# Seven products of quarter matrices for an input projection, with weight sums made by accumulating DMAs

## The chip, the core and the metric

The kernel runs on one NeuronCore of a Trainium2 chip. The metric is the device time of one execution in microseconds (us). Before the change it is 662.69 us, the median of 3 runs (662.54 to 663.6). The profile is one further execution.

TensorE (PE) multiplies: a matmul takes a stationary 128x128 operand, loaded ahead of it, and streams a moving operand of up to 512 columns through it into PSUM. VectorE (DVE), ScalarE (ACT) and GpSimd (POOL) work on tiles in SBUF; the first two can read PSUM as well. DMA queues move data between HBM and SBUF; the queue of SyncE (SP) issues nearly all of them here.

## The reference

One layer over 512 tokens of width 1024, float32. All ten inputs of the two branches and gates come out of one projection of 1024 x 10240:

```python
h = rms_norm(x, norm_gain[layer])
proj = jnp.einsum('bsd,dc->bsc', h, w_in[layer])
(sb_q, sb_k, sb_v, sb_g, r_q, r_k, r_v, r_g, m_sb, m_ret) = jnp.split(proj, SPLIT_POINTS, axis=-1)

qa = rms_norm(split_heads(sb_q, SB_HEADS), sb_q_gain[layer])
ka = rms_norm(split_heads(sb_k, SB_HEADS), sb_k_gain[layer])
va = split_heads(sb_v, SB_HEADS)
out_a = merge_heads(stick_breaking_attention(qa, ka, va)) * jax.nn.silu(sb_g)

qb = rotary(split_heads(r_q, RET_HEADS))
kb = rotary(split_heads(r_k, RET_HEADS)) * (RET_KEY_DIM ** -0.5)
vb = split_heads(r_v, RET_HEADS)
ret = chunkwise_retention(qb, kb, vb)
ret = rms_norm(ret, ret_out_gain[layer][None, :, None, :])
out_b = merge_heads(ret) * jax.nn.silu(r_g)

p_a = jnp.einsum('bsw,wd->bsd', out_a, w_branch_sb[layer])
p_b = jnp.einsum('bsw,wd->bsd', out_b, w_branch_ret[layer])
merged = (jax.nn.sigmoid(m_sb + b_merge[layer, 0]) * p_a
          + jax.nn.sigmoid(m_ret + b_merge[layer, 1]) * p_b)
x = x + jnp.einsum('bsd,de->bse', merged, w_out[layer])
```

## The kernel before, in words

Every large product is computed in three passes: each float32 operand is split into a high part (a copy in the rounded type float32r, on ScalarE) and a low part (the difference, on VectorE), and hi x hi, hi x lo and lo x hi are summed in PSUM (`split`, lines 114 to 116; `mm3`, lines 91 to 95).

The input projection is cut into 20 **groups** of 512 columns: four for queries and keys (`qk`, two heads each), two each for the attention values (`v`), its gate (`sg`), the retention's values (`rv`) and gate (`rg`) and the two merge gates (`ma`, `mb`), and four for the retention's queries and keys (`rqk`, one head each). Six more groups of the same size are the two branch projections (`pa`, `pb`) and the output projection (`fin`). All 26 go through `dense` (line 211): over eight blocks of 128 input rows, four PSUM banks, three passes, so 96 matmuls of 512 columns. `load_split` (line 191) brings the weights in four pieces of 128x1024 per group: a load on SP's queue into one of two raw buffers, a cast on ScalarE and a subtraction on VectorE into one of two pairs of `whi` and `wlo` buffers, all at high priority. The token operand `xT` is made and split once, at the start (line 145).

Attention and retention are generators whose small matmuls are put between those of the groups: `work.step()` in `dense` counts down and resumes them (class `Interleaver`, line 40). So PE's order is fixed by the program; a scheduler orders the other engines by priority, and each engine then runs its instructions in that order.

Behind each group its four PSUM banks are read out: `qk_group` (line 285), `v_group` (line 330), `silu_group` (line 343), `gate_group` (line 357) and `rope_group` (line 429). The calls from line 523 on set the order of the groups.

Of the kernel before, what the change touches and what calls it, by code (L numbers as in the profile page):

```python
# [12 lines left out]
P = 128  # L13
S = 512
# [15 lines left out]
V_ROOM, M_ROOM = 66, 112  # L30


RAW_BUFS = 2
V_BUFS = 14
N_IDLE = 8
# [32 lines left out]
def hybrid_block(ctx, tc, x, x_t, vecs, w_in, w_a, w_b, w_o, cos_t, sin_t, decay, out):  # L68
# [34 lines left out]
    def G_tile(name):  # L103
        return big.tile([P, S], F32, tag="G", bufs=8, name=name)

    def O_pair(name):
        return [big.tile([P, S], F32R, tag="O", bufs=16, name=f"{name}_{q}") for q in range(2)]
# [33 lines left out]
    vec = const.tile([P, V_ROOM], F32, name="vec")[:, :V_N]  # L141
    xT_hi = const.tile([P, NK, S], F32R, name="xT_hi")
    xT_lo = const.tile([P, NK, S], F32R, name="xT_lo")

    def first_loads():

        raws = [wpool.tile([P, 2, S], F32, tag="raw", bufs=RAW_BUFS, name=f"first_raw{k}") for k in range(2)]
        xt = [T_tile(f"xt{hf}", F32) for hf in range(2)]
        for k in range(NK):
            ks = slice(k * P, (k + 1) * P)  # L150
            if k < 4:
                load_weights(raws[k // 2][:, k % 2 : k % 2 + 1, :], w_in, k, 1, ((C_Q, 256), (C_K, 256)))
            load(xt[k // 4][:, k % 4, :], x_t[ks, :])
            if k == 0:
                load(vec, vecs)
        for k in range(NK):
            r = xt[k // 4][:, k % 4, :]
            g = vec[:, V_NG + k : V_NG + k + 1]
            nc.scalar.activation(xT_hi[:, k, :], r, AF.Copy, scale=g)  # L159
            nc.vector.scalar_tensor_tensor(  # L160
                xT_lo[:, k, :], r, g, f32(xT_hi[:, k, :]), op0=ALU.mult, op1=ALU.subtract
            )
        return raws

    first = first_loads()

    idle = const.tile([P, S], mybir.dt.bfloat16, name="idle")
    nc.vector.memset(idle, 0.0)
    pi = side_psum("pi")
    for j in range(N_IDLE):  # L170
        matmul(pi, idle[:, :P], idle, start=True, stop=True)

# [10 lines left out]
    m_half = const.tile([P, M_ROOM], F32, name="m_half")[:, :16]  # L183
# [7 lines left out]
    def load_split(name, w, blocks):  # L191
# [19 lines left out]
    def dense(name, act, w, blocks, rows):  # L211
# [4 lines left out]
        for k, hi, lo in load_split(name, w, blocks):  # L216
            if name == "fin1" and k >= NK - 2:
                late.append((k, act(k), (hi, lo)))
                continue
# [430 lines left out]
```

## Time and profile before

| what | value |
|---|---|
| median of 3 runs | 662.69 us (662.54 to 663.6) |
| the profiled execution, own time | 664.18 us |
| its span, first to last instruction | 662.4 us |
| PE busy / weight loads | 656.3 us (99%) / 546.4 us (82%) |
| VectorE, ScalarE, GpSimd busy | 375.9 us (57%), 260.7 us (39%), 50.8 us (8%) |
| matmuls (PE instructions) | 3096 |
| moved by DMA | 65.02 MB, 98 GB/s in the mean |

The span leaves out 1.78 us of the execution. Matmuls are pipelined and the profile models their ends, so a matmul's own length overlaps its neighbours'; the pace is read from the time that a run of them takes. The view of waits names, for an engine's idle time, what ended last. The chain that ended last follows the program back from its last instruction to what released each step.

### The profile page before, as it was taken

The page shows a single profiled execution, that of the slowest core. Times are in us where ns is not written, and L with a number is a line of the kernel's source. Part 1 is how long each engine was busy: PE and PEld are TensorE (multiplying, and loading weights), DVE is VectorE, ACT ScalarE, POOL GpSimd, SP SyncE. Part 2 cuts the span into 40 slices and gives each one's busy share as a digit, 9 for nine tenths or more (in the row PEclk, how much of TensorE's full clock was granted, in tenths as well). Part 3 has the DMA queues.
Part 4 walks back from the last instruction along what each step waited for, and adds up shares of the span by engine and source line. Part 5 has one row for each costly group of instructions (what it writes and reads, how often), then busy time and mean ns, then how long its engine had stood idle before and what let it go on. Part 6 is the DMA issues. An engine that isn't in the chain of part 4 may idle for free.

```text
span 662.4 us, 7979 instructions
## 1 busy us (share of the span) xinstructions
PE 656.3 (99%) x3096; PEld 546.4 (82%) x3096; DVE 375.9 (57%) x560; ACT 260.7 (39%) x416; POOL 50.8 (8%) x50
## 2 busy tenths in 40 slices
PE   8999999999999999999999999999999999999997
PEld 5888888888888888888888888888888888888886
DVE  6456874587497477632334763844862953544632
ACT  4744534464364554422312342433433443422310
POOL 0051000441000400000000001001001001000000
PEclk9999999999999999999999999999999999999999
DMA  8543223322322323233333323222323322335541
GB/s 288 189 128 96 65 63 96 96 64 65 95 64 64 96 63 96 60 99 96 95 96 111 96 64 106 84 80 81 96 70 106 93 66 64 96 95 161 158 159 63
DMA packets 42182, 65.02 MB, mean 98 GB/s; under 512 B 2848, under 2 KB 19488, under 8 KB 42144
## 3 DMA queue, kind: packets, MB, share of 16 engines
q1 hardware_dynamic: 41568, 63.47, 31.2%
q10 hardware_dynamic: 576, 1.05, 0.4%
q8 instruction: 24, 0.39, 0.3%
q14 instruction: 14, 0.11, 0.1%
HBM read 62.41 MB, written 2.10 MB: 97 GB/s over the span
## 4 chain that ended last, share of the span: by engine, by line
PE 99%; DMA 0%; SPq 0%; ACT 0%; DVE 0%; issue 0%; DVEq 0%; ACTq 0%
PE qk_ps L86 14%; PE rqk_ps L86 13%; PE sg_ps L86 7%; PE v_ps L86 7%; PE ma_ps L86 7%; PE rv_ps L86 7%; PE mb_ps L86 7%; PE rg_ps L86 7%; PE fin_ps L86 7%; PE pb_ps L86 7%; PE pa_ps L86 7%; PE po L86 2%; PE z L86 2%; PE rz L86 2%; PE ro L86 2%; PE pw L89 1%
## 5 line engine op out<-in xcount | busy, mean ns | idle before, releaser
L86 PE MATMUL qk_ps<-qk_hi,xT_hi 128*128 128x512 f32 x128 | 51.5, 411 | 0.9 <-ACT xT_hi L159 0.9
L86 PE MATMUL rqk_ps<-xT_hi,rqk_hi 128*128 128x512 f32 x128 | 50.5, 394 | 0.0
L86 PE MATMUL rqk_ps<-xT_hi,rqk_lo 128*128 128x512 f32 x128 | 50.0, 391 | 0.0
L86 PE MATMUL rqk_ps<-xT_lo,rqk_hi 128*128 128x512 f32 x128 | 50.0, 390 | 0.0
L86 PE MATMUL qk_ps<-qk_lo,xT_hi 128*128 128x512 f32 x128 | 49.8, 398 | 0.0
L86 PE MATMUL qk_ps<-qk_hi,xT_lo 128*128 128x512 f32 x128 | 49.5, 395 | 0.0
L86 PE MATMUL pb_ps<-ob,pb_hi 128*128 128x512 f32 x128 | 39.5, 390 | 0.0
L86 PE MATMUL pa_ps<-oa,pa_hi 128*128 128x512 f32 x128 | 39.4, 389 | 0.0
L116 DVE TENSOR_TENSOR rqk_lo<-rqk_raw,rqk_hi 128x1024 fp32r<-128x1024 f32 x16 | 20.8, 1300 | 23.9 <-ACT rqk_hi L115 23.9
L386 DVE TENSOR_TENSOR_SCAN keep<-keep,zero 128x128 f32<-128x128 f32 (+3 forms) x32 | 27.1, 847 | 7.3 <-ACT keep L384 7.3
L86 PEld LDWEIGHTS qk_ps<-qk_hi,xT_hi 128*128 128x128 f32 x128 | 24.5, 192 | 6.2 <-ACT xT_hi L159 1.8
L86 PEld LDWEIGHTS qk_ps<-qk_hi,xT_lo 128*128 128x128 f32 x128 | 24.5, 191 | 5.4
L189 POOL TENSOR_TENSOR rrr<-ms,m_half 128x4 f32<-128x4 f32 x4 | 4.0, 1007 | 316.3 <-DVE ms L188 316.3
L86 PEld LDWEIGHTS qk_ps<-qk_lo,xT_hi 128*128 128x128 f32 x128 | 24.7, 193 | 4.3
L86 PEld LDWEIGHTS rqk_ps<-xT_hi,rqk_lo 128*128 128x128 f32 x128 | 24.1, 188 | 5.0
L86 PEld LDWEIGHTS pb_ps<-ob,pb_hi 128*128 128x128 f32 x128 | 24.0, 188 | 5.0
L86 PEld LDWEIGHTS pa_ps<-oa,pa_hi 128*128 128x128 f32 x128 | 24.0, 188 | 5.0
L86 PEld LDWEIGHTS rqk_ps<-xT_hi,rqk_hi 128*128 128x128 f32 x128 | 24.1, 188 | 4.7
L86 PEld LDWEIGHTS rqk_ps<-xT_lo,rqk_hi 128*128 128x128 f32 x128 | 24.1, 188 | 4.6
L115 ACT CAST rqk_hi<-rqk_raw 128x1024 fp32r<-128x1024 f32 x16 | 16.8, 1050 | 25.8 <-PE rqk_ps L86 16.5
L116 DVE TENSOR_TENSOR qk_lo<-qk_raw,qk_hi 128x1024 fp32r<-128x1024 f32 x14 | 17.6, 1259 | 15.1 <-ACT qk_hi L115 15.1
L86 PE MATMUL v_ps<-v_hi,xT_hi 128*128 128x512 f32 x64 | 26.1, 408 | 0.0
(185 smaller groups left out, 1709.8 us busy)
## 6 DMA issues: line engine op xcount, KB each, us to landing
rqk_raw<-in_w_in SPq DMA_DIRECT2D x32, 256.0 KB, 3.0
qk_raw<-in_w_in SPq DMA_DIRECT2D x28, 256.0 KB, 3.0
v_raw<-in_w_in SPq DMA_DIRECT2D x8, 512.0 KB, 3.9
sg_raw<-in_w_in SPq DMA_DIRECT2D x8, 512.0 KB, 3.6
rv_raw<-in_w_in SPq DMA_DIRECT2D x8, 512.0 KB, 3.6
ma_raw<-in_w_in SPq DMA_DIRECT2D x8, 512.0 KB, 3.6
pa_raw<-in_w_a SPq DMA_DIRECT2D x8, 512.0 KB, 3.9
rg_raw<-in_w_in SPq DMA_DIRECT2D x8, 512.0 KB, 3.6
```

What stands on the lines that cost most here:

```text
L86: tc.keep_in_program_order(nc.tensor.matmul(*a, **k))
L89: tc.keep_in_program_order(nc.tensor.transpose(*a))
L115: nc.scalar.copy(hi, src)
L116: nc.vector.tensor_sub(lo, src, f32(hi))
L189: nc.gpsimd.tensor_tensor(dst, t[:, :width], m_half[:, :width], op=ALU.pow)
L386: nc.vector.tensor_tensor_scan(keep[:, :n][:, ::-1], keep[:, :n][:, ::-1], zero.broadcast_to([P, n]), 1.0, op0=ALU.mult, op1=ALU.add,)
```

## The change

Each of the 20 projection groups is cut in quarters: token halves (256), input halves (512) and column halves (256). Instead of eight products of quarters, `proj` makes seven products of sums (Strassen's scheme in Winograd's form); each product is 24 matmuls of 256 columns: four blocks of 128 rows, two halves of a PSUM bank, three passes.

- The token sums are made once at the start (`token_operands`): scalings by the norm gain on ScalarE and GpSimd, three sums on GpSimd and one on VectorE, seven splits.
- The weight sums are made for each group in SBUF by DMAs: three quarters are loaded on SP's queue, and four times a quarter is added onto a raw tile by an accumulating DMA that GpSimd issues (`add_from`). One raw tile holds in turn B11, B11+B12, B11+B12+B22 and B11+B12+B22+B21, another B22 and then B22+B12. Each of the seven operands is split into `whi` and `wlo`; there are now three buffers of each and four raw buffers, all 128x1024.
- Sums of products that share a bank go on accumulating in it: ScalarE copies the bank's state out (`kept`, three times a group), and VectorE combines (three times a group). The four result quarters are three SBUF tiles and a PSUM bank.
- The weights come to the chip cut in quarters, each with 4 KB in one piece per partition (`w_q`).
- The functions behind the groups read quarters instead of banks. The split pairs of the branch activations are no longer kept: `branch_act` splits each again for both column halves. The order of groups is changed: `sg1` ahead of `qk2`, both `ma` ahead of both `pa`, `rv0` behind them.

The groups `pa`, `pb` and `fin` keep their 96 matmuls of 512 columns.

```diff
+    def add_from(dst, src):
+        nc.gpsimd.dma_start(dst, src, accum_op=ALU.add)
...
+        s1, s3 = (G_tile(f"xs{j}").rearrange("p a (b t) -> p (a b) t", b=2) for j in range(2))
+        nc.vector.tensor_sub(s1, x21, x22)
+        act_pair("s1", s1)
+        s2, n4 = (G_tile(f"xt{j}").rearrange("p a (b t) -> p (a b) t", b=2) for j in range(2))
+        nc.gpsimd.tensor_sub(s2, s1, x11)
+        act_pair("s2", s2)
+        nc.gpsimd.tensor_add(n4, x12, s2)
+        act_pair("n4", n4)
+        nc.gpsimd.tensor_sub(s3, x11, x21)
...
+    def weight_pair(name, src, by_rows=False):
+        hi = wpool.tile([P, 4, H], F32R, tag="whi", bufs=3, name=f"{name}_hi")
+        lo = wpool.tile([P, 4, H], F32R, tag="wlo", bufs=3, name=f"{name}_lo")
...
+        with tc.high_priority():
+            if g == 0:
+                r = first
+            else:
+                r = raw_tile(f"{name}_raw1")
+                load(r, quarter(g, B11))
+            got = made(0, r)
+        yield got
+        with tc.high_priority():
+            add_from(r, quarter(g, B12))
+            got = made(1, r)
+        yield got
+        with tc.high_priority():
+            add_from(r, quarter(g, B22))
+            r2 = raw_tile(f"{name}_raw2")
+            load(r2, quarter(g, B22))
+            got = made(2, r)
+        yield got
+        with tc.high_priority():
+            got = made(3, r2)
+        yield got
+        with tc.high_priority():
+            add_from(r, quarter(g, B21))
+            add_from(r2, quarter(g, B12))
+            r3 = raw_tile(f"{name}_raw3")
+            load(r3, quarter(g, B21))
+            got = made(4, r2)
+        yield got
...
+    def product(ps, a, b, rows, first):
+
+        for k in range(4):
+            for j in range(2):
+                js, o = slice(j * P, (j + 1) * P), ps[:, j, :]
+                l, r = (a, b) if rows else (b, a)
+                for n, (u, v) in enumerate(((0, 0), (0, 1), (1, 0))):
+                    matmul(
+                        o, l[u][:, k, js], r[v][:, k, :], start=first and k == j == n == 0,
+                        stop=k == 3 and n == 2, skip_group_check=True,
+                    )
+            if k % 2 == 1:
+                work.step()
...
+        y, w = bank("y"), bank("w")
+        product(y, acts["x11"], next(ops), rows, True)
+        c11 = kept("c11", y)
+        product(w, acts["s1"], next(ops), rows, True)
+        c22 = kept("c22", w)
+        product(y, acts["s2"], next(ops), rows, False)
+        c12 = kept("c12", y)
+        product(w, acts["n4"], next(ops), rows, False)
+        nc.vector.tensor_sub(c12, w, c12)
+        product(y, acts["s3"], next(ops), rows, False)
+        with tc.high_priority():
+            nc.vector.tensor_sub(c22, c22, y)
+        q = bank("q")
+        product(q, acts["x12"], next(ops), rows, True)
+        nc.vector.tensor_add(c11, q, c11)
+        product(y, acts["x22"], next(ops), rows, False)
+        return {(0, 0): c11, (0, 1): c12, (1, 0): y, (1, 1): c22}
...
-    def proj(name, blocks, rows):
-        return dense(name, lambda k: (xT_hi[:, k, :], xT_lo[:, k, :]), w_in, blocks, rows)
```

How ScalarE's instructions move is shown at the group `rg0`, the retention's first gate. Before, from its first cast to its last; `rk`, `rm` and the `rqk_hi` made from `rm` are the read-out of the group ahead, `rg_raw` the landed weights:

```order
L115 CAST rg_hi_3067<-rg_raw_3065 128x1024 [waits DMAHW1_49,DVE_49,PE_49]
L436 COPY rk_0_3029<-rqk_ps_2901 128x512 [waits PE_49]
L115 CAST rg_hi_3099<-rg_raw_3097 128x1024 [waits DMAHW3_49,DVE_49,PE_49]
L436 COPY rk_1_3030<-rqk_ps_2902 128x512 [waits PE_49]
L115 CAST rqk_hi_3027<-rm_0_0_3033 128x512 [waits DVE_49]
L115 CAST rqk_hi_3027<-rm_0_2_3035 128x512 [waits DVE_49]
L115 CAST rg_hi_3129<-rg_raw_3127 128x1024 [waits DMAHW4_49,PE_49,Activation_49]
L115 CAST rqk_hi_3027<-rm_1_0_3047 128x512 [waits DVE_49]
L115 CAST rqk_hi_3027<-rm_1_2_3049 128x512 [waits DVE_49]
L115 CAST rg_hi_3181<-rg_raw_3179 128x1024 [waits DMAHW5_49,PE_49,Activation_49]
```

In the change, the same stretch; the digit behind `rg0_` is the operand, DMAHW a load of SP's queue, DMASW a DMA of GpSimd's:

```order
L120 CAST rg0_0_hi_4251<-rg0_raw1_4249 128x1024 [waits DMAHW1_49,DVE_49,PE_49]
L120 CAST rg0_1_hi_4284<-rg0_raw1_4249 128x1024 [waits DMASW0_49,DVE_49,PE_49]
L300 COPY rg0_c11_4281<-rg0_y_4247 128x512 [waits PE_49]
L120 CAST rqk_hi0_4213<-rm0_10_0_4215 128x2x256 [waits DVE_49]
L120 CAST rqk_hi0_4213<-rm0_00_0_4223 128x2x256 [waits DVE_49]
L300 COPY rg0_c22_4312<-rg0_w_4248 128x512 [waits PE_49]
L120 CAST rg0_2_hi_4317<-rg0_raw1_4249 128x1024 [waits DMASW1_49,Activation_49]
L120 CAST rg0_3_hi_4347<-rg0_raw2_4315 128x1024 [waits DMAHW3_49,Activation_49]
L120 CAST rqk_hi0_4213<-rm0_01_0_4231 128x2x256 [waits DVE_49]
L300 COPY rg0_c12_4345<-rg0_y_4247 128x512 [waits PE_49]
L120 CAST rqk_hi0_4213<-rm0_11_0_4239 128x2x256 [waits DVE_49]
L120 CAST rg0_4_hi_4380<-rg0_raw2_4315 128x1024 [waits DMASW3_49,Activation_49]
```

Four casts, each from its own load, have become seven (5 and 6 follow next), of which 1, 2, 4 and 6 stand behind a DMA that GpSimd issues; the copies out of PSUM stand between them.

GpSimd's queue held no DMA. Before, from the last query/key group's scalings to the first of the retention:

```order
L189 TENSOR_TENSOR rr_2011<-ms,m_half 128x16 [waits DVE_49]
L301 TENSOR_TENSOR rr_2011<-rr_2011,rx 128x16 [waits Pool_49]
L303 TENSOR_TENSOR qraw_0_1991<-qraw_0_1991,rr_2011 128x512 [waits PE_49,Activation_49,Pool_49]
L303 TENSOR_TENSOR qraw_1_1993<-qraw_1_1993,rr_2011 128x512 [waits PE_49,Activation_49]
L303 TENSOR_TENSOR qraw_2_1995<-qraw_2_1995,rr_2011 128x512 [waits PE_49,Activation_49]
L303 TENSOR_TENSOR qraw_3_1997<-qraw_3_1997,rr_2011 128x512 [waits PE_49,Activation_49]
L189 TENSOR_TENSOR rrr_3354<-ms,m_half 128x4 [waits DVE_49]
```

In the change, from the second addition of `sg1`, the group behind `qk1`, to the first of the next group:

```order
L154 DMA sg1_raw1_1403<-in_w_q 128x1024 [waits DMASW0_49,DVE_49]
L225 TENSOR_TENSOR rr1_1385<-ms_1390,m_half_169 128x16 [waits DVE_49]
L428 TENSOR_TENSOR rr1_1385<-rr1_1385,rx_171 128x4 [waits Pool_49]
L428 TENSOR_TENSOR rr1_1385<-rr1_1385,rx_171 128x4 x3
L431 TENSOR_TENSOR qraw1_1371<-qraw1_1371,rr1_1385 128x512 [waits Activation_49,Pool_49]
L431 TENSOR_TENSOR qk1_c11_1137<-qk1_c11_1137,rr1_1385 128x512 [waits PE_49,Activation_49,Pool_49]
L431 TENSOR_TENSOR qk1_c12_1227<-qk1_c12_1227,rr1_1385 128x512 [waits Activation_49,Pool_49]
L154 DMA sg1_raw1_1403<-in_w_q 128x1024 [waits DMASW1_49,DVE_49]
L154 DMA sg1_raw2_1469<-in_w_q 128x1024 [waits DMAHW2_49,DMASW7_49,DVE_49]
L431 TENSOR_TENSOR qk1_c22_1183<-qk1_c22_1183,rr1_1385 128x512 [waits Pool_49]
L154 DMA qk2_raw1_1699<-in_w_q 128x1024 [waits DMAHW4_49,DMASW6_49,DVE_49]
```

The additions wait for VectorE's subtractions (DVE) and for earlier additions of their own raw tile (DMASW), and stand in one row with the scalings of the query/key group ahead.

## Rows read from the trace of the kernel before

**Rows 1.** The page: span, busy time by engine, granted clock in 40 slices.

```profile
span 662.4 us, 7979 instructions
...
PE 656.3 (99%) x3096; PEld 546.4 (82%) x3096; DVE 375.9 (57%) x560; ACT 260.7 (39%) x416; POOL 50.8 (8%) x50
...
PEclk9999999999999999999999999999999999999999
```

**Rows 2.** The page: the chain that ended last, shares of the span by engine.

```profile
PE 99%; DMA 0%; SPq 0%; ACT 0%; DVE 0%; issue 0%; DVEq 0%; ACTq 0%
```

**Rows 3.** Groups of PE instructions by form: count, busy us, mean ns, idle us before.

```profile
L86 PE MATMUL qk_ps<-qk_hi,xT_hi 128*128 128x512 f32 x128 | 51.5, 411 | 0.9 <-ACT xT_hi L159 0.9
...
L86 PE MATMUL rqk_ps<-xT_hi,rqk_lo 128*128 128x512 f32 x128 | 50.0, 391 | 0.0
```

**Rows 4.** The chain in order of time: start us, length us, what.

```profile
53.38 4.08 PE sg_ps L86 x18
...
276.08 21.76 PE pa_ps L86 x96
...
363.12 12.24 PE rg_ps L86 x54
...
396.74 2.52 PE ro L86 x21
...
571.41 43.52 PE pb_ps L86 x192
```

**Rows 5.** Groups of ScalarE and VectorE instructions by form.

```profile
L116 DVE TENSOR_TENSOR rg_lo<-rg_raw,rg_hi 128x1024 fp32r<-128x1024 f32 x8 | 9.8, 1222 | 6.8 <-ACT rg_hi L115 6.8
...
L544 DVE TENSOR_TENSOR pa<-pa_ps,ma 128x512 f32<-128x512 f32 x8 | 5.5, 692 | 2.6 <-PE pa_ps L86 2.6
...
L115 ACT CAST rg_hi<-rg_raw 128x1024 fp32r<-128x1024 f32 x8 | 8.4, 1052 | 13.6 <-PE rqk_ps L86 8.8 <-PE rg_ps L86 4.9
...
L486 ACT COPY roraw<-ro 128x512 f32<-128x512 f32 x8 | 4.7, 585 | 23.7 <-PE ro L86 23.7
```

**Rows 6.** Timeline of one weight split in `rg`: start us, us, engine, what.

```profile
373.85 1.05 ACT L115 CAST rg_hi<-rg_raw 128x1024 fp32r<-128x1024 f32 x1 [1.24 <-PE rg_ps L86]
...
374.94 1.22 DVE L116 TENSOR_TENSOR rg_lo<-rg_raw,rg_hi 128x1024 fp32r<-128x1024 f32 x1 [1.60 <-ACT rg_hi L115]
```

**Rows 7.** DMA issues: count, KB each, median us from issue to landing.

```profile
rqk_raw<-in_w_in SPq DMA_DIRECT2D x32, 256.0 KB, 3.0
...
rg_raw<-in_w_in SPq DMA_DIRECT2D x8, 512.0 KB, 3.6
...
x<-in_x SPq DMA_DIRECT2D x2, 1024.0 KB, 8.6
```

**Rows 8.** Groups of GpSimd instructions by form.

```profile
L303 POOL TENSOR_TENSOR qraw<-qraw,rr 128x512 f32<-128x512 f32 x16 | 19.2, 1227 | 0.3
L189 POOL TENSOR_TENSOR rr<-ms,m_half 128x16 f32<-128x16 f32 x4 | 13.6, 3391 | 152.2 <-DVE ms L188 152.2
```

**Rows 9.** Two stretches: busy us of engines, granted clock, DMA share, GB/s.

```profile
6.00:12.00 6.00, 6.00 (x19) 4.74 (x19) 5.07 (x10) 2.90 (x5) 0.00 (x0) 1.00 0.96 341
...
363.00:580.00 217.00, 217.00 (x1056) 183.56 (x1055) 129.27 (x184) 82.79 (x118) 12.18 (x12) 1.00 0.28 84
```

**Rows 10.** Waits: engine, line, waited for; us in total, times, longest us.

```profile
ACT pb_hi L115 <- PE pb_ps L86: 17.5, 5, 4.4
```

**Rows 11.** Timeline of the start: the last split of a first weight piece.

```profile
10.94 0.69 DVE L205 TENSOR_TENSOR qk_lo<-first_raw,qk_hi 128x512 fp32r<-128x512 f32 x1
```

More of the change, by code (lines that the diff above doesn't have):

```diff
@@ L139, in hybrid_block, with raw_tile, quarter @@
     nc.scalar.activation(warm, zero, AF.Sigmoid)
[L141 to L167, printed above, removed]
+    vec = const.tile([P, V_N], F32, name="vec")
+    def raw_tile(name):
+        return wpool.tile([P, 4, H], F32, tag="raw", bufs=RAW_BUFS, name=name)
+    def quarter(g, q):
+        return w_q[g, q].rearrange("p (k c) -> p k c", k=4)
+    def add_from(dst, src):
+        nc.gpsimd.dma_start(dst, src, accum_op=ALU.add)
+    xt = [T_tile(f"xt{hf}", F32) for hf in range(2)]
+    first = raw_tile("first_raw")
+    load(vec, vecs)
+    for k in range(4):
+        load(first[:, k, :], quarter(0, B11)[:, k, :])
+        load(xt[0][:, k, :], x_t[k * P : (k + 1) * P, :])
+    load(xt[1], x_t[4 * P :, :].rearrange("(k p) t -> p k t", p=P))
+    idle = tmp.tile([P, 2 * S], mybir.dt.bfloat16, tag="tmp", name="idle")[:, :S]
     nc.vector.memset(idle, 0.0)
@@ L201, in load_split @@
[L201 to L207 removed]
+                raw = raw_tile(f"{name}_raw{k}").rearrange("p (a b) c -> p a (b c)", a=2)
+                load(raw, w[k * P : (k + 2) * P, c0 : c0 + S].rearrange("(a p) c -> p a c", p=P))
@@ L475, in retention @@
             yield 1
-        vv = v()
         for b2 in range(2):
@@ L533, in hybrid_block @@
-    sg[1] = silu_group("sg1", C_G + S)
-    qk_group(3)
-    work.add(attention((6, 7), lambda: 1 in sg, lambda: v[1], lambda: sg[1]))
-    rv[0] = v_group("rv0", C_RV)
-    pa = []
-    for g in range(2):
-        m = gate_group(f"ma{g}", C_MA + S * g, V_BM + 4 * g)
-        ps = dense(f"pa{g}", branch_act(oa), w_a, ((S * g, S),), False)
-        t = T_tile(f"pa{g}", F32)
+    sg[1] = silu_group("sg1", 4)
+    qk_group(2, 5)
+    work.add(attention((4, 5), lambda: 1 in sg and 1 in v, lambda: v[1], lambda: sg[1]))
@@ L543, in hybrid_block @@
+    v[1] = v_group("v1", 6)
+    qk_group(3, 7)
+    work.add(attention((6, 7), lambda: 1 in sg and 1 in v, lambda: v[1], lambda: sg[1]))
+    pa = [gate_group(f"ma{n}", 8 + n, V_BM + 4 * n) for n in range(2)]
+    for n in range(2):
+        ps = dense(f"pa{n}", branch_act(f"oa{n}", oa), w_a, S * n, False)
         for j in range(4):
-            nc.vector.tensor_mul(t[:, j, :], ps[j], m[j])
-        pa.append(t)
-    def ret(h):
-        rq = rope_group(h)
+            nc.vector.tensor_mul(pa[n][:, j, :], ps[j], pa[n][:, j, :])
```

372 lines of the change are left out of this document (217 added, 155 removed).

## Prediction

> **What bounds the kernel now.** I read the page's engine shares first, then the chain that ended last, then that chain in order of time. TensorE (PE) is busy 99% of the 662.4 us span at the full granted clock, 9 tenths in every slice [rows 1], and the chain lies on it for 99% [rows 2]: nothing but PE time counts today. The chain in order of time gives the price of a projection group: 96 matmuls of 512 columns take 21.76 us, 226.7 ns each [rows 4]. (The mean in the table of groups, 391 ns, is a modelled length of overlapping instructions, and no pace [rows 3].) The same view has a run of 256-column matmuls: 21 in 2.52 us, 120 ns each [rows 4]. So 256 columns more cost 106.7 ns, which leaves 13.3 ns that each matmul costs whatever its width.
>
> Next come the waits: ScalarE's casts wait for PE to give weight buffers back, 4.4 us at a time [rows 10]. Weights are ready early now, and the whole margin of the forecast is whether they still are. Last, the side work (attention, retention) between the groups. From 53.38 to 276.08 eight groups stand, 8 x 21.76 = 174.1 of 222.7 us: 6.1 us of side work each. From 363.12 to 571.41 eight more: 174.1 of 208.3, 4.3 us each [rows 4].
>
> **The change, part by part.** *PE.* Seven products of 24 matmuls replace 96 matmuls. A product is 24 x 120 ns = 2.88 us, a group 20.16 us: 1.60 us less, 32 us over 20 groups. An eighth of the columns would be 2.7 us; the 13.3 ns on 72 more matmuls takes back the rest. The six groups of the branch and output projections stay at 21.76.
>
> *ScalarE and VectorE.* A group has seven casts of 128x1024 where it had four, each 1.05 us, and seven subtractions at 1.22 [rows 5]; three copies out of PSUM at about 0.59 and three combinations at about 0.69 [rows 5]. The branch activations are split for each half of the columns, 16 more pairs. VectorE: 376 us [rows 1] + 60 x 1.22 + 60 x 0.69 + 16 x 0.69 = 501; ScalarE 261 + 63 + 35 + 10, less 12 copies that go (7), 362. Neither fills 640 us, so I cost them at nothing as throughput. They count as links in a chain.
>
> *The chain of a weight operand.* An accumulating DMA overwrites the quarter that was just split, so it may start only behind that split's subtraction, and the next cast starts only when it has landed. Call its time, from subtraction's end to landing, L. A cast and its subtraction take 2.31 us (373.85 to 376.16) [rows 6]; I take s = 2.55, since four times a group such a step queues behind VectorE work of around 0.7 us. Number the products 0 to 6. Operand n takes the buffer of operand n - 3, so operand 0 of a group waits for product 4 of the group before. From there:
> - **X**, from the end of product 4 to the start of the next group's product 2: split 0, add, split 1, add, split 2 = 3s + 2L. PE has products 5, 6, 0 and 1 to cover it, 11.52 us, and four sevenths of the side work.
> - **Y**, from the start of product 2 to that of product 4: operand 3 is a plain load, its subtraction ends 1.25 later, then add and split: 1.25 + s + L, against 5.76 us of products and two sevenths.
> - **Z**, product 4: 2.88 us and a seventh.
>
> The order of the instructions bears this out: cast 1 of a group stands on ScalarE right behind cast 0 with a wait for the DMA between, and the four additions go through GpSimd's queue in a row.
>
> *L.* No row of before shows an accumulating DMA. The nearest row is the plain load of the same 512 KB, 3.6 us [rows 7]. An addition reads its destination too. The table of DMA issues has 256 KB in 3.0 us and 512 KB in 3.6, so another 512 KB of reading is some 1.2 us: L = 4.8, my value. From below, a gain against 3.6 isn't excluded: the new layout gives each partition one 4 KB piece, where the loads of before go in pieces of 2 KB or 1 KB, and such a piece may travel better; I take 3.2. From above, a 1024 KB load lands in 8.6 us, at the crowded start [rows 7]. I keep to 4.8 because the stages in question are not crowded: from 363 to 580 the DMA engines are busy 28% at 84 GB/s, and they have reached 341 [rows 9].
>
> With L = 4.8, X = 17.25 and Y = 8.6. The covers with side work of 6.1 are 15.0 and 7.5; with 4.3, 14.0 and 7.0; with none, 11.5 and 5.8: the chain is later in every group. Group times are X + Y + Z: 29.6 in eight attention groups (237), 29.35 in eight retention groups (235), 28.75 in two without side work (58). The group behind the two pa projections finds its first operands made, and takes 11.5 + 8.6 + 2.9 = 23.
>
> *Start.* The first raw quarter is split by about 11 us (the last such subtraction ends at 11.6 now, twice as wide) [rows 11]. Then two additions and splits, Y and a product: 11 + 2(L + s) + 8.6 + 2.9 = 37.2 to the end of product 4. The sums of token quarters run beside it: four scalings on GpSimd at 1.23 or less [rows 8], a subtraction and a split end near 19, before the weights of product 2.
>
> *GpSimd.* Its queue now holds the additions among the query/key scalings: a power of 3.4 us and three products of 1.23 [rows 8] stand between the second and third addition of the groups behind the first two query/key groups. They end about when that third addition is wanted; I count nothing, and 2 us for each of the two go into the range.
>
> *Sum.* 37.2 + 237 + 235 + 58 + 23, products 5 and 6 of the last group (5.8), six unchanged groups (130.6), the tail behind the last matmul (3.9): 730 us of span, about **731** with the 1.8 us that this execution takes outside its span. That is 67 above the profiled 664.18, itself 1.5 above the median of 662.69; that difference lies in the range.
>
> By the Trainium skill (DMA: Bandwidth & Descriptors, Anatomy of one DMA) a DMA issued from GpSimd takes 2.0 us plus its bytes at 436 GB/s; an estimate by it is 3.2 us for 512 KB. The page's formula is for a plain DMA; no run here shows one from that engine, and the sum by it would be 650.
>
> **The rivals.** *1, faster: the additions land as quickly as a good load.* Each us of L is worth 58 us (three links in 18 groups, one in the group behind pa, three at the start). L = 3.6 gives 663, so that is the point: below it the change wins. At 3.2 the attention groups are bound by PE alone (15.0 + 7.5 + 3.75 = 26.25), the retention groups take 24.55, those without side work 24.0: 210 + 196 + 48 + 21.4 + 32.4 + 140.3 = 648, **650** with the rest. With no wait at all it would be 640. For it: the longer pieces and the idle DMA engines. Against it: the second stream that an addition reads.
>
> *2, slower still: an addition is far from a load,* through descriptors made by GpSimd's software or an adder below the engines' copy rate. L = 6 gives **801**, 8.6 gives 951. For it: nothing in these rows limits it; against it: the 28% DMA load.
>
> *3, the clock falls.* PE's only idle time in the main groups now is 0.9 us at the start [rows 3], and the clock stays at 2.4 GHz [rows 1]. The forecast leaves PE idle twice a group for 1 to 6 us. If the grant drops to 1.2 GHz, the 106.7 ns per matmul double: 2.6 us on a product. Product 4 is the one with no cover: 18 x 2.6 = 46, **777**. The Trainium skill (TensorE: Matmul & The Clock Gate, The HAM clock gate) has the throttled clock as the default that activity releases, which speaks against this change; the trace has no idle stretch long enough to agree or differ.
>
> *4, nothing moves:* stalls and the 32 us cancel (L near 3.6), **663**.
>
> **How the numbers follow.** Forecast, L between 3.7 and 5.6, 668 to 778: 0.46. Rival 1: 0.18. Rival 2: 0.20. Rival 3: 0.11. Rival 4: 0.05. The measurement can tell 0.2%, 1.3 us. Faster 0.18, same 0.05, slower 0.77. The range goes from 650, rival 1 at 3.2, to 850, where L would be 6.9: outside lie the best part of rival 1 and the far end of rival 2, about 0.2. The slower cases' own range is 668 to 850.
>
> **What would show it.** Right: PE's share near 88%, its idle time at the first matmul of products 2 and 4, released by ScalarE's cast or VectorE's subtraction; in the chain that ended last, GpSimd's DMAs with a share of a quarter or more; additions landing in 4 to 6 us; 256-column matmuls 120 ns apart inside a product. Wrong: an addition landing in under 3.6 us with PE still at 97% or more (rival 1); additions of 6 us and more (rival 2); a granted clock under 0.95 (rival 3); a pace above 120 ns, which would upset the 20.16; or stalls that end on a free PSUM or SBUF buffer, which I cost at nothing.

## The result, and the profile after

The changed kernel takes **877.35 us** (median of 4 runs, 874.45 to 878.61) against 662.62 for the kernel before: ratio 1.323, 95% interval 1.320 to 1.327. The forecast was 731, its range ended at 850. The direction was right, the size was not: 146 us are missing from the sum.

The page of the changed kernel: engine shares, PE and its granted clock in 40 slices, the GpSimd queue's share of the DMA engines, the chain that ended last, and the two kinds of 512 KB transfer (median us from issue to landing).

```profile
span 876.8 us, 11443 instructions
...
PE 707.8 (81%) x4536; PEld 656.5 (75%) x4536; DVE 500.8 (57%) x748; ACT 354.2 (40%) x583; POOL 142.2 (16%) x149
...
PE   4676797858978679699977868969778778888997
...
PEclk7686988979898799999998979979889897999999
...
q0 software_dynamic: 11520, 41.95, 27.8%
...
DMA 34%; PE 25%; issue 15%; DVE 12%; ACT 7%; POOL 6%; POOLq 0%; SPq 0%; ACTq 0%; DVEq 0%
...
rqk_raw<-in_w_q POOLq DMA_DIRECT2D x16, 512.0 KB, 5.4
...
rqk_raw<-in_w_q SPq DMA_DIRECT2D x12, 512.0 KB, 3.7
```

Where the chain was PE for 99% [rows 2], it now runs through DMAs for 34%, PE for 25%. PE falls from 99% [rows 1] to 81%, with stalls in nearly every slice, and the granted clock, 9 tenths throughout before, dips in most. VectorE's 500.8 us and ScalarE's 354.2 are the forecast's 501 and 362.

One group step by step, rqk0 to rg0, first ScalarE's casts of weights, then GpSimd's issues, both from the timeline (start, length, what ended the idle time before).

```profile
457.01 1.05 ACT L120 CAST rqk_hi<-rqk_raw 128x1024 fp32r<-128x1024 f32 x1 [3.82 <-PE rv_y L88]
...
464.99 1.05 ACT L120 CAST rqk_hi<-rqk_raw 128x1024 fp32r<-128x1024 f32 x1 [1.74 <-DMA rqk_raw<-in_w_q]
...
473.05 1.99 ACT L120 CAST rqk_hi<-rqk_raw 128x1024 fp32r<-128x1024 f32 x2 [2.18 <-DMA rqk_raw<-in_w_q]
...
483.52 2.94 ACT L120 CAST rqk_hi<-rqk_raw 128x1024 fp32r<-128x1024 f32 x3 [2.77 <-DMA rqk_raw<-in_w_q]
490.19 1.05 ACT L120 CAST rg_hi<-rg_raw 128x1024 fp32r<-128x1024 f32 x1 [3.73 <-PE rqk_y L88]
```

```profile
459.67 0.86 POOL L154 DMA_DIRECT2D rqk_raw<-in_w_q  x1 [15.28 <-DVE rqk_lo L121]
467.65 0.88 POOL L154 DMA_DIRECT2D rqk_raw<-in_w_q  x1 [7.11 <-DVE rqk_lo L121]
475.70 0.88 POOL L154 DMA_DIRECT2D rqk_raw<-in_w_q  x1 [7.17 <-DVE rqk_lo L121]
476.84 0.86 POOL L154 DMA_DIRECT2D rqk_raw<-in_w_q  x1 [0.26 <-issue]
```

This is the chain that the forecast drew. Cast 0 waits for product 4 (457.01). Its subtraction ends at 459.33, the addition is issued 0.34 us later and cast 1 can start at 464.99: L, from the subtraction to the cast that the landing releases, is 5.65 us, within 0.1 us the same at the second link, and 6.97 at the third, where the addition for operand 4 (476.84) stands behind one that only operand 6 needs (475.70). The stretches X, Y and Z of this group, as windows (from the end of product 4 to the end of split 2, to that of split 4, to the end of the next product 4; the bounds, then busy us of each engine, granted clock, DMA share, GB/s):

```profile
457.01:475.35 18.34, 12.79 (x98) 11.89 (x96) 8.31 (x14) 8.40 (x14) 1.75 (x2) 0.93 0.48 107
475.35:485.83 10.48, 8.11 (x48) 7.71 (x48) 3.06 (x4) 2.89 (x4) 1.74 (x2) 0.80 0.56 100
485.83:490.15 4.32, 4.27 (x23) 4.27 (x24) 2.27 (x2) 0.64 (x1) 0.00 (x0) 0.60 0.67 216
```

Forecast: 17.25, 8.6 and 3.5. In Z the clock is at 0.60 of 2.4 GHz: most of its matmuls start 213 ns apart instead of 120.

To compare kernels over all groups, I took X, Y and Z from the timeline by the starts of the first matmuls of products 2, 4 and 5 (18 groups; the first and the one behind pa left out; here side work that lies between two products counts to the stretch before it). A product's first matmul needs only the cast, so these bounds can lie 1.2 us ahead of those of the windows. Means in us:

```
                              X      Y      Z     sum   whole kernel
forecast                    17.25   8.6    3.55  29.4     731
changed kernel              19.4   11.35   4.9   35.7     877.35
e4 the same program again   19.1   11.1    4.8   35.1     866.0
e1 plain copies, GpSimd     16.2    9.1    4.65  30.0     761.86
e2 plain copies, SP         15.5    8.1    4.6   28.3     731.73
e3 no chain                 14.5    6.85   4.9   26.2     687.98
e5 PE kept busy             20.7   11.9    4.35  36.9     899.44
e8 VectorE adds two         14.9    7.2    4.9   27.1     704.90
e17 order of additions kept 22.75  12.1    4.9   39.8     946.91
```

The runs e1 to e11 and e17 are single runs. e4, described below, turned out to be the changed program once more, in the series of e1 to e3: against it the gains of these three are 11 us smaller than against 877.35.

The three links of the same 18 groups, from the subtraction's end to the landing, means in us:

```
                            first  second  third
forecast                     4.8    4.8     4.8
changed kernel               6.0    5.9     7.8
e4 the same program again    5.8    5.6     7.7
e1 plain copies, GpSimd      4.3    4.0     5.5
```

### The profile page after: what moved, and what is told of

Its sections match the earlier page's. It is cut to its first block, busy times and chain, and to the rows that moved or that the text cites. A ratio compares the mean times of both kernels' runs of the same rounds, so it can differ in the third digit from the quotient of the medians.

```text
span 876.8 us, 11443 instructions
## 1 busy us (share of the span) xinstructions
PE 707.8 (81%) x4536; PEld 656.5 (75%) x4536; DVE 500.8 (57%) x748; ACT 354.2 (40%) x583; POOL 142.2 (16%) x149
## 4 chain that ended last, share of the span: by engine, by line
DMA 34%; PE 25%; issue 15%; DVE 12%; ACT 7%; POOL 6%; POOLq 0%; SPq 0%; ACTq 0%; DVEq 0%
DMA qk_raw<-in_w_q 6%; DMA rqk_raw<-in_w_q 6%; PE fin_ps L88 5%; PE pb_ps L88 5%; DMA rg_raw<-in_w_q 4%; PE pa_ps L88 4%; DMA v_raw<-in_w_q 3%; DMA rv_raw<-in_w_q 3%; DMA ma_raw<-in_w_q 3%; DMA mb_raw<-in_w_q 3%; DMA sg_raw<-in_w_q 3%; DVE qk_lo L121 2%; PE qk_y L88 2%; PE sg_y L88 1%; DVE rqk_lo L121 1%
## 5 line engine op out<-in xcount | busy, mean ns | idle before, releaser
L120 ACT CAST qk_hi<-qk_raw 128x1024 fp32r<-128x1024 f32 x24 | 24.6, 1048 | 39.3 <-DMA qk_raw<-in_w_q 30.5
L88 PE MATMUL rqk_y<-s_hi,rqk_hi 128*128 128x256 f32 x64 | 23.8, 372 | 17.8 <-ACT rqk_hi L120 13.1
L121 DVE TENSOR_TENSOR rv_lo<-rv_raw,rv_hi 128x1024 fp32r<-128x1024 f32 x14 | 17.5, 1276 | 26.0 <-ACT rv_hi L120 26.0
L88 PEld LDWEIGHTS rqk_y<-s_hi,rqk_hi 128*128 128x128 f32 x64 | 17.3, 270 | 19.5 <-ACT rqk_hi L120 14.1
L121 DVE TENSOR_TENSOR v_lo<-v_raw,v_hi 128x1024 fp32r<-128x1024 f32 x14 | 18.2, 1333 | 21.5 <-ACT v_hi L120 21.5
L88 PEld LDWEIGHTS pb_ps<-ob,pb_hi 128*128 128x128 f32 x128 | 24.6, 194 | 7.8 <-DVE mb L707 2.7
L121 DVE TENSOR_TENSOR sg_lo<-sg_raw,sg_hi 128x1024 fp32r<-128x1024 f32 x14 | 16.7, 1223 | 20.4 <-ACT sg_hi L120 20.4
L121 DVE TENSOR_TENSOR mb_lo<-mb_raw,mb_hi 128x1024 fp32r<-128x1024 f32 x14 | 17.4, 1275 | 18.8 <-ACT mb_hi L120 18.8
L121 DVE TENSOR_TENSOR ma_lo<-ma_raw,ma_hi 128x1024 fp32r<-128x1024 f32 x14 | 17.6, 1276 | 16.0 <-ACT ma_hi L120 15.9
L88 PE MATMUL rqk_y<-s_hi,rqk_lo 128*128 128x256 f32 x64 | 23.9, 373 | 3.5 <-DVE rqk_lo L121 3.5
L88 PE MATMUL qk_y<-qk_hi,s_hi 128*128 128x256 f32 x64 | 23.1, 360 | 3.3 <-ACT qk_hi L120 3.3
```

The source lines that it names most:

```text
L88: tc.keep_in_program_order(nc.tensor.matmul(*a, **k))
L120: nc.scalar.copy(hi, src)
L121: nc.vector.tensor_sub(lo, src, f32(hi))
```

## The experiments

My theory after this reading: the links of the chain are long because the transfer adds. Rivals: its issue by GpSimd, GpSimd's own work ahead of it in the queue, the sharing of the engines by two additions, and the clock.

**Plain copies in place of the additions.** In `add_from`:

```diff
-        nc.gpsimd.dma_start(dst, src, accum_op=ALU.add)
+        nc.gpsimd.dma_start(dst, src)     (e1)
+        nc.sync.dma_start(dst, src)       (e2)
```

> The four adding transfers of a group become plain copies of the same 512 KB, still issued by GpSimd with the same waits (so the sums of weight quarters are left out and the operands are single quarters). In the changed kernel a link from the end of the subtraction to the landing took 5.65, 5.65 and 6.97 us, and three links lie on the path of each of 19 groups, so 1 us less per link is worth 57 us. Theory 'the adding is slow': links fall to the 3.3 to 4.7 us of a plain load issued by SP, 750 to 810 us. Rival 'issue by GpSimd and two transfers sharing the engines': the links stay within 0.5 us, 850 to 880 us.

> The same plain copies with the same data waits, issued by SP instead (sums left out). The chain stands, each link about 3.6 to 4.2 us, nothing waits behind GpSimd's own work. Theory 'length of the links': about 1.6 us less on two links and 2.8 us on the third, 6 us per group, 19 groups, 114 us off: 700 to 770 us, and near 690 if the clock rises as well. Rival 'clock' (the stalls, however short, keep TensorE at half speed): over 800 us. If SP's queue, which now waits with the loads behind it, is what binds: over 800 too, but then with SP's waits in the chain.

e1 takes 761.86 us: with the same waits, the same issuer and the same bytes fetched, 115 us go when nothing is added (104 against e4). The transfer lands in 3.5 us instead of 5.4, and GpSimd's issue takes 0.53 us instead of 0.87 (e1's DMA issues and GpSimd's groups by form):

```profile
rqk_raw<-in_w_q POOLq DMA_DIRECT2D x16, 512.0 KB, 3.5
...
L154 POOL DMA_DIRECT2D rqk_raw<-in_w_q x16 | 8.5, 531 | 106.2 <-DVE rqk_lo L121 105.3 <-DVE wT L121 1.0
```

The links become 5.9 us a group shorter, 107 us over 18 groups, which is nearly all of the gain. The third stays the longest, so adding is not its only cause. e2 takes 731.73: the way through GpSimd, its queue and its issue together, is worth 30 us more. 69 us above the kernel before remain.

**The transfers alone.** The computation is left out; transfers of four sizes and three kinds follow one another.

> The whole computation is left out; in its place 64 transfers follow one another, four of each, each waiting for the last: a plain load by SP, a plain load by GpSimd and an adding load by GpSimd, of 128, 256, 512 and 1024 KB, and then two adding loads of 512 KB issued together. From the kernels run so far, 512 KB took 3.2 to 3.3 us by SP, 3.6 by GpSimd and 5.4 adding. Theory 'adding moves bytes at a lower rate': the adding load is level with the plain one at 128 KB (within 0.5 us) and its lead in time grows with the size, to some 3.5 us at 1024 KB. Rival 'adding has a fixed price per transfer': 1.8 us more at every size. Of the two together, by sharing: the first lands no earlier than about 7, the second by about 9 us; by queueing: the first at 5.5, the second near 9.

The DMA issues of that kernel: sp is a plain load by SP, gp one by GpSimd, add the adding one (KB, median us to landing).

```profile
sp<-in_w_q SPq DMA_DIRECT2D x4, 1024.0 KB, 4.6
gp<-in_w_q POOLq DMA_DIRECT2D x4, 1024.0 KB, 4.9
add<-in_w_q POOLq DMA_DIRECT2D x4, 1024.0 KB, 8.0
two<-in_w_q POOLq DMA_DIRECT2D x8, 512.0 KB, 6.2
sp<-in_w_q SPq DMA_DIRECT2D x4, 512.0 KB, 3.1
gp<-in_w_q POOLq DMA_DIRECT2D x4, 512.0 KB, 3.5
add<-in_w_q POOLq DMA_DIRECT2D x4, 512.0 KB, 5.1
...
gp<-in_w_q POOLq DMA_DIRECT2D x4, 256.0 KB, 2.9
add<-in_w_q POOLq DMA_DIRECT2D x4, 256.0 KB, 3.7
...
gp<-in_w_q POOLq DMA_DIRECT2D x4, 128.0 KB, 2.6
add<-in_w_q POOLq DMA_DIRECT2D x4, 128.0 KB, 3.1
```

Adding costs 0.5 us at 128 KB, 0.8 at 256, 1.6 at 512, 3.1 at 1024: the price grows with the size and is not a fixed one. From 512 to 1024 KB an adding load needs 2.9 us more, which is 181 GB/s; a plain one 1.4. Of two additions issued together the first is read 5.2 us after the issue begins and the second 8.1: they queue, the first is not slowed. By the Trainium skill (DMA: Bandwidth & Descriptors, Anatomy of one DMA) 512 KB from GpSimd are an estimated 3.2 us; the plain load's 3.5 here is near it, the adding load's 5.1 is not, and the measurement decides.

**No chain.** Each of the operands 1 to 6 has its own tile, plainly loaded.

```diff
-            add_from(r, quarter(g, B12))
-            got = made(1, r)
+                t = raw_tile(f"{name}_raw{j + 1}")
+                load(t, quarter(g, q))
+                got = made(j, t)
```

> Operands 1 to 6 each have a raw tile of their own, filled by one plain load with no wait on an earlier operand (sums left out; seven loads and no additions per group). Theory 'the chain of additions is all that costs': TensorE runs through, groups of 20.2 to 21 us, clock near 0.98, start about as long as in the changed kernel's less two links: 640 to 680 us. Rival 'the casts, subtractions and recombinations bind' (VectorE is busy 501 us as in the changed kernel): over 720 us.

687.98 us, 8 above the expected range: all that waits for additions is worth 189 us (178 against e4), and yet this kernel without any sum of weights is still 25 us above the kernel before. The longest of its PE waits (us in total, times, longest) are for token sums at the start and for GpSimd's scalings of queries and keys; e11 below tests whether these are the whole rest.

```profile
PE pqk L91 <- POOL qk_c L411: 12.7, 4, 7.0
PE qk_w L88 <- ACT s_hi L120: 8.1, 1, 8.1
```

**The clock.** Twenty matmuls of zeros ahead of products 2 and 4:

```diff
+        keep_busy()
         product(y, acts["s2"], next(ops), rows, False)
```

> Twenty matmuls of 256 columns of zeros (bf16, 0.11 us each at 2.4 GHz, 2.1 us together) stand on TensorE ahead of products 2 and 4 of every group, in a bank that product 5 clears later; all else as in the changed kernel. Theory 'chain, with the clock on product 4 alone': the dummies lie in the stalls, product 4 runs at 2.4 GHz (Z 4.3 to 3.1 us in the group looked at) and nothing else on the path changes: about 1.2 us on 19 groups, 23 us off, 845 to 862 us, the clock above 0.95. Rival 'the clock sets the time' (0.89 of full speed over the whole run, 11% of it): 800 us or less. Rival 'the stalls are shorter than the dummies': no gain or slower, 875 to 890 us.

899.44 us, above every expected range. The mean granted clock rises from 0.89 to 0.94 and Z falls by 0.6 us per group, but X and Y rise by 1.2 and 0.6. By this run the clock in product 4 is worth some 10 us (18 x 0.57). What it costs elsewhere is not separated here; but a kernel with a higher clock and the same additions is no faster, so the clock is not the main cause.

**GpSimd's queue.** First its scalings were moved to VectorE (`nc.gpsimd.tensor_tensor` to `nc.vector.tensor_tensor` in two places), then the last two additions swapped.

> The scalings of queries and keys (16 of 128x512) and of the retention's outputs (8) go from GpSimd to VectorE; the two kinds of power stay on GpSimd. Theory 'GpSimd's own work ahead of the additions holds them up': two query and key groups by 4 to 7 us each, three retention groups by 1 to 3 us: 15 to 25 us off, 852 to 862 us. Rival 'other additions are late anyway, and VectorE's extra 0.7 us stand in the chain instead': 870 to 885 us.

> Nothing but the order of the last two additions is swapped: the one that operand 4 waits for is issued ahead of the one that only operand 6 needs. Theory 'the two share the engines, and the first issued lands first': the third link falls from 6.97 to about 5.7 us, 1.2 to 1.4 us on 19 groups: 848 to 856 us. Rival 'the landing is long whichever is first' (the link was long for GpSimd's work ahead of it): 870 to 880 us. But the addition that now goes first waits for the subtraction of operand 3, 1.1 us later, and the other waits behind it; that costs nothing while operand 6 has over 5 us to spare.

e6: 862.51. e4: 866.0, but the scheduler had put the two additions back, so that e4 is the changed kernel once more, 1.3% below the first four runs. The 3.5 us between e6 and e4 are the most that can be claimed for the scalings, and less than the 1.3% between two measurements of one program; what does show is that in `v0` and `sg1`, behind the first two query/key groups, Y fell from 14.7 and 15.1 in e4 to 12.4 and 13.1. The swap was then fixed in program order, and with it the place of all four additions of a group among GpSimd's instructions:

```diff
-        nc.gpsimd.dma_start(dst, src, accum_op=ALU.add)
+        tc.keep_in_program_order(nc.gpsimd.dma_start(dst, src, accum_op=ALU.add))
...
-            add_from(r, quarter(g, B21))
             add_from(r2, quarter(g, B12))
+            add_from(r, quarter(g, B21))
```

> The swap of the last two additions again, now also in the order in which GpSimd issues them (in the earlier run of this edit the scheduler put them back, and every engine's instructions stood as in the changed kernel; its 866.0 us are a second measurement of that kernel). Transfers alone showed two additions of 512 KB issued together landing after 5.2 and 8.1 us: the first is not slowed, the second queues. Theory 'the third link is long for standing second in the queue': Y (product 2 to product 4) falls from 11.1 to 11.4 us by 1.3 to 2, 24 to 36 us over 18 groups: 830 to 845 us. Rival 'the link is long for something else': Y stays, 860 to 880 us.

946.91 us, and both sides of it show. In 14 of the 18 groups the third link is now 5.4 to 6.1 us, like the other two: standing second in the queue is what made it longer. Y falls with it in the retention groups without GpSimd work in the way: rg0 12.1 (10.8 in e4) to 9.1, rg1 10.7 to 9.1, mb0 10.6 to 9.3. In rqk1, rqk2, rqk3 and mb1 Y rises to 20.2, 22.1, 20.1 and 21.7, since the kept order leaves the addition for operand 4 behind the retention's power, which waits for VectorE (GpSimd's timeline):

```profile
658.66 0.87 POOL L154 DMA_DIRECT2D rqk_raw<-in_w_q  x1 [8.01 <-DVE wT L121]
677.82 1.03 POOL L225 TENSOR_TENSOR rrr<-ms,m_half 128x4 f32<-128x4 f32 x1 [18.29 <-DVE ms L224]
678.93 2.04 POOL L623 TENSOR_TENSOR roraw<-roraw,rrr 128x512 f32<-128x512 f32 x2
680.91 1.82 POOL L154 DMA_DIRECT2D rqk_raw<-in_w_q  x2
```

Product 4 waits for the addition, the retention's next steps wait for PE, and the power waits for them.

The larger loss is in X. In v0, sg1, v1 and ma0, the groups behind query/key groups, it rises from 17.3 to 24.6 us in the changed kernel to 34.3 to 38.6, 66 us in all: the kept order puts their first addition behind the power and the scalings of the group ahead. For v0 it is issued at 66.70 where the changed kernel had 52.44, and PE waits up to 17.7 us for cast 1 (GpSimd's timeline; PE's waits):

```profile
59.14 2.90 POOL L225 TENSOR_TENSOR rr<-ms,m_half 128x16 f32<-128x16 f32 x1 [7.60 <-DVE ms L224]
...
63.72 3.04 POOL L431 TENSOR_TENSOR qk_c<-qk_c,rr 128x512 f32<-128x512 f32 x3
66.70 0.88 POOL L154 DMA_DIRECT2D v_raw<-in_w_q  x1
```

```profile
PE v_w L88 <- ACT v_hi L120: 32.7, 2, 17.7
```

One queue's order costs 70 us and more.

**The sums elsewhere.** Four tiles per group; VectorE adds B12 and B22 onto B11, and the two remaining additions stay on DMAs, off the chain:

```diff
-            add_from(r, quarter(g, B12))
+            nc.vector.tensor_add(r, r, t12)
+            add_from(t12, quarter(g, B22))
...
-            add_from(r, quarter(g, B22))
+            nc.vector.tensor_add(r, r, t22)
```

> All seven operands as in the changed kernel, but no adding transfer stands between two operands: each group loads B11, B12, B22 and B21 into four tiles (one more plain load); VectorE adds B12 and then B22 onto B11 (two additions of 128x1024, some 1.22 us each by the subtractions of that shape), and the DMAs add B22 onto B12's tile (operand 4, from the first addition on, no longer behind operand 3) and B21 onto the running sum (operand 6, one product earlier to spare). Theory 'the chain of additions is what costs': as the kernel without additions, 688 us, plus little: 680 to 705 us. Rival 'VectorE binds' (501 + 49 = 550 us busy, and GpSimd's or the DMAs' work beside it): 720 us or more. Rival 'adding transfers slow the loads beside them': 705 to 730.

> The kernel before this one in the list, with two more edits: at the start the scaling of the second half of the tokens and the first two sums of tokens go from GpSimd (6.2, 3.2 and 3.2 us) to VectorE (about 2, 1.2 and 1.2); and the transposes of a query and key group wait for 12 half products instead of 8, since TensorE stood 12.7 us for GpSimd's scalings in the kernel with no chain. Theory: the start falls by 8 to 10 us, the waits on the scalings by 10 us: 18 to 22 us below the kernel before it, 660 to 685 us. Rival 'the work that was behind the transposes comes late instead': less than 10 us.

> The kernel with VectorE adding B12 and B22 (704.9 us) with three edits: the start's scalings and first two sums on VectorE as before (they brought the first group's last product from 46.6 to 39.1 us), the transposes at 8 half products again, the query, key and retention scalings on VectorE, and the retention's first scores two half products later (TensorE stood 2 to 3 us for the cast of its operand, four times). Theory 'these are separate stalls on TensorE's path': 7.5 + 7 + 8 us off, 680 to 687 us. Rival 'VectorE, then 560 us busy, is late elsewhere instead': 690 to 705. Under 660 would beat the kernel before; neither theory has it.

> The kernel with seven plain loads and no sums of weights (688.0 us), with the start's scalings and two sums and all scalings of queries, keys and retention on VectorE. It says what is left if the sums of weights cost nothing at all. Theory 'start and scalings are what it lost to the kernel before': 7.5 and 12.7 us off, and some 5 us for the clock after those stalls: 663 to 670 us, level with the kernel before. Rival 'seven products with their recombinations leave TensorE more, once it does not wait': 640 to 655 us.

e8, with every sum made, takes 704.90: the chain of additions was the main cost, 172 of the 215 us. It lies at the edge of the rival by which adding transfers slow the loads beside them, and this run doesn't exclude it for the 17 us that e8 is above e3. e9 shortened the start as expected (first group's last product at 39.1 us, before that 46.6) and came out slower, 714.67 against an expected 660 to 685: with the transposes put off, the attention ran over into pa (70 us from pa's first matmul to the next group's where e8 had 48). e10: 689.39, between its theory and its rival. e11, with no sums of weights at all: 679.26, against an expected 663 to 670; so the start and the scalings were not the whole rest, and what the remaining 17 us are stays open. Seven products for all twenty groups lose to the kernel before in this program even with free sums; but e10's nine groups from rqk0 to pb took 215.6 us, those of the kernel before 230.1.

**Seven products for the second half only.** The first ten groups whole, as before the change; rv0 to mb1 as in e10. Five kernels differ in where the sums of token quarters are made.

> The first ten groups are computed whole, as in the kernel before (eight products' worth of matmuls in 512 columns), and only the last ten, rv0 to mb1, by seven products, with the sums of e10 (VectorE adds B12 and B22, the DMAs the other two). The token operands s1, s2 and n4 are made by GpSimd from the split tokens during the first groups, s3 between the two attention matmuls. From rqk0 to the first matmul of pb the kernel before took 230.1 us (341.2 to 571.3), e10 took 215.6 (375.3 to 590.9). Theory 'seven products pay where nothing waits for sums, start or scalings': 14 us for these nine groups and 1.6 for rv0, less some 6 us that e10's pb is longer than before's: 650 to 657 us, ratio 0.981 to 0.991. Rival 'what the first half gained from rv0's place or loses by GpSimd's sums ahead of the first query scalings is as much': 658 to 668 us, ratio about 1.

> The kernel before it (668.6 us), with one edit: GpSimd's sums of tokens wait for the end of the second group (v0), and so stand behind the scalings of the first queries and keys instead of ahead of them. In that kernel sg0 began at 67.9 us against 53.2 in the kernel before: 6 us were lost in qk0 and 9 in v0, while from rv0 (334.5) to the first matmul of pb (570.2) it took 235.8 us, where the kernel before takes 251.8 for rv0's 21.8 and the nine groups' 230.1. Theory 'GpSimd's sums beside the start's splits, and ahead of the scalings, cost those 15 us': 653 to 658 us, ratio 0.985 to 0.993, below both kernels. Rival 'the start is late for its layout or its loads, not for GpSimd': 664 to 669 us, ratio 1.000 to 1.008.

> The kernel before it (669.4 us), with one edit: the casts and subtractions that split the three sums of tokens move from ScalarE and VectorE to GpSimd, which makes the sums. In that kernel ScalarE stood 9.4, 3.4 and 6.3 us in front of these casts in sg0, with the attention's sigmoids behind them, and sg0 took 41.4 us against 27.6 in the kernel before. Theory 'waiting for GpSimd in ScalarE's order is what cost 14 us': sg0 falls to 28 to 31 us, the whole to 654 to 659 us, ratio 0.986 to 0.994. Rival 'VectorE runs slower beside GpSimd (a scan of 384 took 2.04 us there, 0.96 without) and that sets sg0': 662 to 668 us.

> The first ten groups whole and the last ten by seven products, as in the three kernels before, with two edits against the first of them: the sums of tokens are made by VectorE (13 operations, 0.7 to 1.2 us each) and split by ScalarE and VectorE, after the first queries' and keys' power, so GpSimd does nothing beside them; and behind each pb the four products with the gate come ahead of the additions and splits, so that its banks come free sooner (pb1 stood 2.3 us for them). Theory 'GpSimd's sums are what the first half lost, by slowing VectorE and by waits in order': the last group of the first half ends 8 to 14 us earlier than 335.6, and pb gives 3 back: 651 to 657 us, ratio 0.981 to 0.990, below both kernels. Rival 'the first half loses for its order of groups or its buffers': 661 to 667 us.

> As the kernel before it (first ten groups whole, last ten by seven products, sums of tokens by VectorE, 663.2 us), with one edit: the sums of tokens are made between the two attention matmuls pa0 and pa1, where VectorE has little else, instead of in the second group. In that kernel sg0 began at 57.9 us (before: 53.2), the group after it at 92.7 (80.8), TensorE stood 5.5, 3.6 and 1.1 us for VectorE there, and rv0 began at 331.7. Theory 'the first half lost only what making the sums in it cost': sg0 at 53 to 54 us, rv0 at 319 to 323, from there to pb 235.8 as before: 650 to 656 us, ratio 0.980 to 0.988, below both kernels. Rival 'the sums are late for rv0 instead, or make pa1 wait': 657 to 662.

```
                                                            us     ratio (95%)
e12 GpSimd, before v0                                     668.57   1.0055 to 1.0094
e13 GpSimd, behind v0                                     669.43   1.0066 to 1.0128
e14 GpSimd, casts and subtractions too                    666.61   1.0027 to 1.0056
e15 VectorE, in v0; pb's four gate products ahead         663.17   0.9974 to 1.0014
e16 VectorE, between pa0 and pa1                          651.81   0.9812 to 0.9854
```

All five take 235.8 us from rv0 to pb, 16 less than the same ten groups in the kernel before (251.8). The first four lost that again in whatever group made the sums, and missed their expectations (650 to 657, 653 to 658, 654 to 659, 651 to 657). In e13 ScalarE, in its order, waits for GpSimd's sum with the attention's sigmoids behind it, and VectorE runs slower beside GpSimd (timelines of ScalarE, GpSimd and VectorE):

```profile
67.06 1.05 ACT L120 CAST s_hi<-xs 128x1024 fp32r<-128x1024 f32 x1 [9.35 <-POOL xs L231]
```

```profile
79.34 3.29 POOL L237 TENSOR_TENSOR xs<-xs,xT_hi 128x512 f32<-128x512 f32 x2 [2.42 <-DVE s_lo L121]
```

```profile
79.51 2.04 DVE L614 TENSOR_TENSOR_SCAN keep<-keep,zero 128x384 f32<-128x384 f32 x1
...
96.68 0.96 DVE L614 TENSOR_TENSOR_SCAN keep<-keep,zero 128x384 f32<-128x384 f32 x1
```

The same scan takes 2.04 us while GpSimd adds and 0.96 when it doesn't. The Trainium skill (SBUF — State Buffer, SBUF: two separate sides) has the two engines share a pair of ports, the loser waiting for the whole instruction, where an instruction of VectorE has two inputs in SBUF, as this scan has; the trace agrees. e14 takes the waits out of ScalarE's order and gains 3 us where 10 to 15 were expected: by this run they were not the main loss. Its rival, VectorE slowed beside GpSimd, fits (662 to 668 expected, 666.61 measured).

e16 puts the sums between two groups without attention or retention and is **1.7% faster than the kernel before**, 26% below the change. Its page:

```profile
span 649.9 us, 9752 instructions
...
PE 640.4 (99%) x3816; PEld 567.4 (87%) x3816; DVE 477.6 (73%) x719; ACT 315.5 (49%) x513; POOL 58.0 (9%) x62
...
PE   8989999999999999999999999999999999999997
...
PEclk9999999999999999999999999999999999999999
```

From the first matmul of rg0 to that of pb it takes 361.93 to 557.39, 195.5 us for eight groups; the kernel before took 208.3 [rows 4]. That is 1.60 us a group, the very term of the forecast; rv0 and rqk0, without side work, take 20.15 and 20.16 us.

## Why the prediction was wrong, step by step

- **The pace** (a product 2.88 us, a group 1.60 us less): right, by e16, once PE does not wait.
- **The throughput of VectorE and ScalarE**: right as sums. Whether VectorE costs nothing is open: e8 is 17 us above e3 with two more additions a group on VectorE, 545 us busy, but it also has adding transfers beside its loads, and no run separates the two.
- **The chain, its three links and what releases them**: right; every wait of PE in the group shown is for a cast or a subtraction of this chain, as the forecast has it (it also stands 0.5 and 0.8 us at product 1).
- **L = 4.8 for all three links**: the step that failed. The forecast took 1.2 us for the bytes that an addition reads more, from the slope of plain loads between 256 and 512 KB [rows 7]. The adding transfer does not move at that slope: 181 GB/s between 512 and 1024 KB, 5.4 us to landing in the kernel, and with the 0.3 us to its issue the link is 5.65. The third link is 6.97, as the addition for operand 4 queues behind another, which the forecast saw in GpSimd's order and gave no price. In the group shown that is 2 x 0.85 + 2.17 = 3.9 us; casts and subtractions of 2.31 for 2.55 give 1.0 back. Over the 18 groups the links are 6.0, 5.9 and 7.8 us: 5.3 us a group too much, 95 us in all, more than half of it in the third.
- **Z with a seventh of the side work**: too small, 4.9 us for 3.5. In 9 of the 18 groups the granted clock in Z is 0.50 to 0.76 of 2.4 GHz; in the others Z is 2.9 to 5.5 us, by the side work that falls to it. Up to 0.9 us in a group are a stall behind the first matmul, which the forecast has in Y. e3 has 4.9 too, but two of its groups wait 7.0 and 5.1 us there for GpSimd's scalings; its other sixteen have 3.9.
- **GpSimd's own work costed at nothing**: too little. In v0 and sg1 the addition for operand 4 is issued 4.1 us after its data are ready, behind the scalings, and the third link is 11.5 and 11.2 us; in other groups these delays are under 2 us. What the queue can cost when its order is less lucky is e17.
- **Start**: 37.2 us forecast for the end of the first product 4, 49.6 measured. The first addition took 8.9 us among the first loads, and GpSimd's token sums of 128x1024 took 2.4 to 3.4 us each. They did not only run beside it: product 1's weights were split at 21.5 us, its token sum's cast ended at 23.7.
- **Sum**: 112 us in the 18 groups (6.2 each) and 12 at the start. From ma1 over pa to rv0 it took 81.9 us for 66.5, 10 of these 15 us in products 5 and 6 of ma1 with the side work left over (10.5 for 5.8) and in pa (48.6 for 43.5). The end, from mb1's product 5 on, took 103.2 for 96.7.
- **The rivals**: 2 was the right one. The mean link of 6.6 us gives 833 by the forecast's own 58 us for each us of L, so L alone does not reach 877. Rival 3 came with it instead of apart from it: the clock is 0.89 in the mean. The range treated L, the clock, the start and GpSimd's queue one by one; all were on the same side, and the range ended at an L of 6.9 with nothing else wrong.

## What to carry to other kernels

A sum made by a DMA is a transfer with a latency: put it on a chain between two uses and its landing counts; made ahead of time in a tile of its own, twice a group in e16, it leaves PE 99% busy. Price a transfer that adds by its own measurement, not by a plain load. When multiplications are saved, look for the part of the program in which the engines that must make the sums have room, and make them there.

## What the runs showed of the hardware that was not expected

An adding load of 512 KB takes 5.1 us alone, a plain one from the same engine 3.5; the difference grows with the size (0.5 us at 128 KB, 3.1 at 1024). GpSimd is busy 0.87 us issuing it, 0.53 for a plain one. Two issued together land one after the other (5.2 and 8.1 us). The granted clock fell to 1.2 GHz twice in the group shown: in a stall of PE of 3.9 us ahead of product 2, and again behind stalls of 1.6 and 0.8 us at product 4, where matmuls of 256 columns then start 213 ns apart. In e17 an addition stood in GpSimd's order behind a power that waited 18.3 us for VectorE. Two measurements of the changed program, with every engine's instructions in the same order, differ by 1.3% (877.35 and 866.0); why is not known.
